# Low parts of thirty weight blocks moved from GpSimd to VectorE at the borders of phases

## Chip, cores and metric

The kernel runs on one core of a Trainium2 chip. The metric is the device time of one execution in microseconds (us); lower is better.

## The reference, cut to what matters

A decoder trunk of two layers on 512 tokens of width 1024 in float32. Each layer is a half-step SwiGLU feed-forward ("ffn"), a token mixer, and a second ffn; every one of the six sub-layers is wrapped in a norm ahead and a norm behind:

```python
h = rmsnorm(x, g[0])
x = x + 0.5 * rmsnorm(swiglu(h, wg, wu, wd), g[1])   # swiglu: (silu(h @ wg) * (h @ wu)) @ wd, 2816 wide
h = rmsnorm(x, g[2])
...                                                  # mixer: z = h @ w_in; scan, gating; y @ w_out
x = x + rmsnorm(y, g[3])
h = rmsnorm(x, g[4])
x = x + 0.5 * rmsnorm(swiglu(h, wg2, wu2, wd2), g[5])
```

## The kernel before

**Split weights.** TensorE multiplies in fp32r, so each operand is split in a high and a low part and a product is three matmuls (high times high, and the two mixed ones). The weights come in blocks of 128x1024. `WeightStream` takes them in one fixed order over the whole kernel: a DMA from SP's queue into one of 4 raw buffers (`load_to`), a cast to `whi` on ScalarE and a subtraction `wlo = raw - whi` (`split`, lines 86 and 87), into one of 8 pairs of buffers (`NW`). The set `early` says for which blocks the subtraction is made by GpSimd; for the others it is VectorE. `prep_to(n)` makes everything up to block n. In three of the ffn phases most gate and up weights come as sevenths of a fast 2x2 scheme; for these blocks VectorE also forms the differences `T` (lines 108 to 119) ahead of the split.

**Phases.** `PLAN` has six: ffn 0/0, mix0, ffn 0/1, ffn 1/0, mix1, ffn 1/1. The 512 tokens are four chunks of 128. A phase ends in `tail` or `out_late` and then `finish`: the output product is summed for one chunk after the other (`some`), and as soon as a chunk is summed its `chain` runs: `post_norm` (a sum of squares on ScalarE, a reciprocal root on VectorE, the residual), then `pre_norm` for the next phase, whose result is `xn`. `rstd` is the reciprocal root: seven instructions on 128x1 columns (lines 450 to 458). `turn` transposes `xn` on TensorE, casts it to `hT_hi` on ScalarE and subtracts to `hT_lo` on VectorE.

**Borders.** The turns of chunks 1 and 2 are put between the last matmuls for chunk 4. Those of chunks 3 and 4 are handed to the next phase as `self.late`. There `lead` makes the first three pairs of weight blocks for tokens 0 to 255 (chunks 1 and 2), turns chunk 3 after the first pair and chunk 4 ahead of the sixth block, and then makes tokens 256 to 511. mix0 has no lead: it makes the gating product of chunk 1, turns chunk 3, goes on with chunk 2 and another product of chunk 1, and turns chunk 4. A paired ffn then forms sums of quarters of `hT` on VectorE (`left_factors`; the last is S3, written back into `hT_lo`).

**Order.** A scheduler orders each engine's instructions by the order in which they are written and by a simulated timeline; each engine then runs its list in order. In the tails TensorE's list is as written. `with tc.issue_after(ins)` adds for each instruction inside, if it is on the same engine as `ins`, that it stands behind `ins` in that engine's list. It leaves the other engines' instructions free.

Of the kernel before, what the change touches and what calls it, by code (L numbers as in the profile page):

```python
# [15 lines left out]
ALU = mybir.AluOpType  # L16
# [13 lines left out]
NW = 8  # L30
# [18 lines left out]
class WeightStream:  # L49
# [4 lines left out]
    def __init__(self, nc, raw_pool, w_pool):  # L54
        self.nc, self.raw_pool, self.w_pool = nc, raw_pool, w_pool
        self.blocks, self.items = [], []
        self.loaded = 0
        self.ready = 0
        self.raw = {}
        self.hi = {}  # L60
        self.lo = {}
        self.t_pool = None
# [327 lines left out]
class Trunk:  # L390
    def __init__(self, ctx, tc, a, out):
        self.ctx, self.tc, self.nc, self.a, self.out = ctx, tc, tc.nc, a, out
        nc = self.nc
        ent = ctx.enter_context
        self.cp = ent(tc.tile_pool(name="cp", bufs=1))
        self.raw_pool = ent(tc.tile_pool(name="rawp", bufs=NRAW))
        self.w_pool = ent(tc.tile_pool(name="wp", bufs=NW))
        self.gp = ent(tc.tile_pool(name="gp", bufs=1))
        self.tp = ent(tc.tile_pool(name="tp", bufs=2))
        self.sp = ent(tc.tile_pool(name="sp", bufs=4))  # L400
        self.ps = ent(tc.tile_pool(name="ps", bufs=4, space=PSUM))

        self.first = {}
        self.ws = WeightStream(nc, self.raw_pool, self.w_pool)
        for ph in PLAN:
            self.first[ph] = len(self.ws.items)
            self.phase_blocks(ph, self.ws)
        self.ws.early = {v + k for v in self.first.values() for k in range(2, 8)} | {0, 1}
        self.ws.early |= {self.first[PLAN[1]] + k for k in range(12, 18)}

        self.x = self.cp.tile([P, NT, D], F32, tag="x", name="x")
        self.hi = self.cp.tile([P, KC, S], F32R, tag="hT_hi", name="hT_hi")
        self.lo = self.cp.tile([P, KC, S], F32R, tag="hT_lo", name="hT_lo")
# [99 lines left out]
    def pre_norm(self, c, gain, nm, cut=D):  # L513

        nc = self.nc
        xn = self.tp.tile([P, D], F32, tag="t", name=f"xn{nm}_{c}")
        ss = self.sumsq(self.x[:, c, :], xn, f"{nm}b{c}")
        r = self.rstd(ss, 1.0 / D, EPS, f"{nm}b{c}")
        nc.vector.scalar_tensor_tensor(xn[:, 0:cut], self.x[:, c, 0:cut], r, gain[:, 0:cut], ALU.mult, ALU.mult)
        if cut < D:  # L520
            nc.gpsimd.tensor_scalar(xn[:, cut:], self.x[:, c, cut:], r, None, ALU.mult)
            nc.gpsimd.tensor_mul(xn[:, cut:], xn[:, cut:], gain[:, cut:])
        return xn
# [55 lines left out]
    def finish(self, acc, some, n, mid, after, ph, nxt, nm):  # L579

        nc, ws = self.nc, self.ws
        xn = {}

        def chain(c):
            self.post_norm(c, acc[c], self.g_post, ph[0] == "ffn", nm, nxt is None)
            if nxt is not None:
                xn[c] = self.pre_norm(c, self.g_pre, nm)

        for c in range(3):
            some(c, 0, n)  # L590
            if c < 2:
                chain(c)
        j = 0
        for c, to in enumerate(mid):
            some(3, j, to)
            if nxt is not None:
                self.turn(c, xn[c], nm)
            if c == 0:
                chain(2)
            j = to  # L600
        some(3, j, n)
        ws.prep_to(after + 4)
        chain(3)
        if nxt is not None:
            self.late = [lambda: self.turn(2, xn[2], nm), lambda: self.turn(3, xn[3], nm)]
# [51 lines left out]
    def lead(self, first, nm, sink, pairs=LEAD):  # L657

        nc, ws = self.nc, self.ws
        w, pg = [], []  # L660
        for i in range(pairs):
            w += [ws.get(first + j, first + j + 1) for j in range(2 * i, 2 * i + 2)]
            pg.append(self.bank2(f"lead{nm}_{i}"))
            if i == 0:
                wh, wl = (v.rearrange("p (k f) -> p k f", f=P) for v in w[0])
                for n, (s, m) in enumerate(((wh, self.hi), (wl, self.hi), (wh, self.lo))):
                    for k in range(KC):
                        nc.tensor.matmul(pg[0][:, 0, 0:256], s[:, k], m[:, k, 0:256],
                                         start=n == k == 0, stop=n == 2 and k == KC - 1)
            else:  # L670
                self.chmajor(pg[i][:, 0], w[2 * i], 0, 256)
            if i == 0:
                self.chmajor(pg[i][:, 1], w[1], 0, 256)
                self.late[0]()
            elif i == pairs - 1:
                with self.tc.issue_after(self.late[1]()):
                    self.chmajor(pg[i][:, 1], w[2 * i + 1], 0, 256)
            else:
                self.chmajor(pg[i][:, 1], w[2 * i + 1], 0, 256)
        for i in range(pairs):  # L680
            ws.prep_to(first + 2 * i + NW)
            for j in range(2):
                self.chmajor(pg[i][:, j], w[2 * i + j], 256, 512)
                ws.drop(first + 2 * i + j)
            sink(i, pg[i])
        ws.prep_to(first + 2 * pairs - 2 + NW)
# [886 lines left out]
```

## Time and profile before

| | |
|---|---|
| median of 3 runs | 1900.11 us (1899.27 to 1902.82) |
| profiled execution | 1899.38 us |
| its span, first to last instruction | 1897.6 us |
| mean granted clock of TensorE | 0.985 of 2.4 GHz |

Engines: PE is TensorE's matmul, PEld its weight load, DVE is VectorE, ACT ScalarE, POOL GpSimd, SP SyncE, whose queue starts the weight loads. L87 is line 87. A row of a timeline gives start and length in us, engine, line, operation, output and inputs, and in brackets how long its engine was idle before it and what ended that.

### The profile page before, as it was taken

The numbers are of one execution on the slowest core, as the hardware profiler recorded it, in microseconds if no ns is written. First come the engines' busy times: TensorE is split into PE (matmuls) and PEld (weight loads), VectorE is DVE, ScalarE is ACT, GpSimd is POOL, SyncE is SP. The second block draws the span as 40 slices with busy tenths as digits, with TensorE's granted clock in tenths as the row PEclk, the third lists the DMA queues.
The fourth block names the chain that finished last, engine by engine and source line by source line (L and its number), as shares of the span: only waits on it lengthen the run. The fifth ranks groups of instructions, "written<-read, shape, count | busy, mean of one in ns | idle before, by whom it ended". The sixth has DMA issues, their size and how long they took to land.

```text
span 1897.6 us, 27701 instructions
## 1 busy us (share of the span) xinstructions
PE 1837.0 (97%) x11192; PEld 1638.0 (86%) x11192; DVE 1220.2 (64%) x1814; ACT 701.1 (37%) x946; POOL 302.0 (16%) x530
## 2 busy tenths in 40 slices
PE   8999999989898999999989999999999989999998
PEld 8888888869787999988889999888988779999886
DVE  5756434284948888853598887428634598887533
ACT  4223224133233544442234444323444334444420
POOL 6037760031402000000110000003122030000000
PEclk9999999989999999999999999999999999999999
DMA  6444432342402233343223335332311132334411
GB/s 224 132 120 147 129 117 89 89 155 92 142 23 89 81 109 112 108 151 98 57 77 91 112 101 166 100 89 81 111 45 45 45 101 88 103 101 133 123 56 45
DMA packets 59602, 193.34 MB, mean 102 GB/s; under 512 B 6577, under 2 KB 13745, under 8 KB 59473
## 3 DMA queue, kind: packets, MB, share of 16 engines
q1 hardware_dynamic: 50544, 182.48, 31.3%
q10 hardware_dynamic: 7680, 5.24, 0.9%
q0 software_dynamic: 1248, 3.84, 0.6%
q8 instruction: 88, 1.44, 0.3%
q14 instruction: 42, 0.34, 0.1%
HBM read 182.10 MB, written 9.44 MB: 101 GB/s over the span
## 4 chain that ended last, share of the span: by engine, by line
PE 89%; DVE 8%; issue 1%; ACT 1%; DMA 0%; DVEq 0%; SPq 0%; ACTq 0%
PE accffn L645 16%; PE accffn L647 8%; PE guffn L543 4%; PE guffn L545 4%; PE guffn L544 4%; PE saffn L848 3%; PE sbffn L848 3%; PE sbffn L847 3%; PE sbffn L849 3%; PE saffn L849 3%; PE saffn L847 3%; PE scffn L848 3%; PE scffn L849 3%; PE scffn L847 3%; PE accmix L645 2%; PE leadffn L544 2%
## 5 line engine op out<-in xcount | busy, mean ns | idle before, releaser
L86 ACT CAST whi<-raw 128x1024 fp32r<-128x1024 f32 x314 | 328.9, 1050 | 610.7 <-PE accffn L647 192.9
L87 DVE TENSOR_TENSOR wlo<-raw,whi 128x1024 fp32r<-128x1024 f32 x270 | 331.8, 1229 | 292.2 <-ACT whi L86 291.7
L87 POOL TENSOR_TENSOR wlo<-raw,whi 128x1024 fp32r<-128x1024 f32 x44 | 106.9, 2454 | 980.7 <-ACT whi L86 971.6
L543 PE MATMUL guffn<-hT_hi,whi 128*128 128x512 f32 x352 | 141.0, 401 | 0.0
L545 PE MATMUL guffn<-hT_hi,wlo 128*128 128x512 f32 x352 | 138.8, 394 | 0.0
L544 PE MATMUL guffn<-hT_lo,whi 128*128 128x512 f32 x352 | 138.1, 392 | 0.0
L848 PE MATMUL saffn<-hT_lo,whi 128*128 128x256 f32 x432 | 122.1, 283 | 0.0
L849 PE MATMUL saffn<-hT_hi,wlo 128*128 128x256 f32 x432 | 122.0, 282 | 0.0
L847 PE MATMUL saffn<-hT_hi,whi 128*128 128x256 f32 x432 | 121.2, 281 | 0.0
L86 ACT CAST whi<-T 128x1024 fp32r<-128x1024 f32 x81 | 85.0, 1050 | 85.9 <-PE saffn L848 43.9
L87 DVE TENSOR_TENSOR wlo<-T,whi 128x1024 fp32r<-128x1024 f32 x81 | 98.9, 1221 | 8.9 <-ACT whi L86 8.9
L545 PE MATMUL leadffn<-hT_hi,wlo 128*128 128x256 f32 x352 | 100.3, 286 | 0.0
L544 PE MATMUL leadffn<-hT_lo,whi 128*128 128x256 f32 x352 | 100.2, 285 | 0.0
L543 PE MATMUL leadffn<-hT_hi,whi 128*128 128x256 f32 x352 | 100.0, 287 | 0.0
L847 PEld LDWEIGHTS saffn<-hT_hi,whi 128*128 128x128 f32 x432 | 82.0, 190 | 0.1
L849 PEld LDWEIGHTS saffn<-hT_hi,wlo 128*128 128x128 f32 x432 | 81.2, 188 | 0.0
L848 PEld LDWEIGHTS saffn<-hT_lo,whi 128*128 128x128 f32 x432 | 80.8, 187 | 0.1
L545 PEld LDWEIGHTS guffn<-hT_hi,wlo 128*128 128x128 f32 x352 | 66.1, 188 | 17.0
L544 PEld LDWEIGHTS guffn<-hT_lo,whi 128*128 128x128 f32 x352 | 66.1, 188 | 15.3
L543 PEld LDWEIGHTS guffn<-hT_hi,whi 128*128 128x128 f32 x352 | 66.1, 188 | 15.0
L543 PEld LDWEIGHTS leadffn<-hT_hi,whi 128*128 128x128 f32 x352 | 67.6, 193 | 0.0
L544 PEld LDWEIGHTS leadffn<-hT_lo,whi 128*128 128x128 f32 x352 | 67.6, 192 | 0.0
(797 smaller groups left out, 5097.2 us busy)
## 6 DMA issues: line engine op xcount, KB each, us to landing
raw<-in_gu_dram SPq DMA_DIRECT2D x108, 512.0 KB, 3.6
raw<-in_wd_dram SPq DMA_DIRECT2D x88, 512.0 KB, 3.6
raw<-in_wg_dram SPq DMA_DIRECT2D x34, 512.0 KB, 3.6
raw<-in_wu_dram SPq DMA_DIRECT2D x34, 512.0 KB, 3.8
raw<-in_even_in_dram SPq DMA_DIRECT2D x12, 512.0 KB, 3.7
raw<-in_odd_tm_dram SPq DMA_DIRECT2D x12, 512.0 KB, 3.6
raw<-in_even_out_dram SPq DMA_DIRECT2D x8, 512.0 KB, 4.4
raw<-in_odd_cm_dram SPq DMA_DIRECT2D x8, 512.0 KB, 3.5
```

Source lines behind the costliest of these rows:

```text
L86: nc.scalar.copy(hi, raw)
L87: (nc.gpsimd if i in self.early else nc.vector).tensor_sub(lo, raw, hi.bitcast(F32))
L543: nc.tensor.matmul(out, sh, mh, start=start, stop=False)
L544: nc.tensor.matmul(out, sh, ml, start=False, stop=False)
L545: return nc.tensor.matmul(out, sl, mh, start=False, stop=stop).ins
L645: nc.tensor.matmul(acc[:, h, :], gh, w[:, h * 512:(h + 1) * 512], start=first, stop=False)
L647: nc.tensor.matmul(acc[:, h, :], gl, wh[:, h * 512:(h + 1) * 512], start=False, stop=stop)
L847: nc.tensor.matmul(o, wh[:, q], ah[k], start=start and k == 0, stop=False, skip_group_check=True)
L848: nc.tensor.matmul(o, wh[:, q], al[k], start=False, stop=False, skip_group_check=True)
L849: nc.tensor.matmul(o, wl[:, q], ah[k], start=False, stop=stop and k == 3, skip_group_check=True)
```

## The change

The set of blocks whose low part GpSimd makes shrinks to the first eight of the kernel and six later ones of mix0; in the five other phases the blocks 2 to 7 go to VectorE. `pre_norm` keeps its last instruction, the one that writes `xn`, in `self.normed`. `finish` prepares six blocks of the next phase, not four, and its VectorE instructions stand behind the `xn` that was written last, which is that of chunk 3; after the last phase it prepares none. `lead` does the same for the blocks behind its first six, behind `xn` of chunk 4.

```diff
-        self.ws.early = {v + k for v in self.first.values() for k in range(2, 8)} | {0, 1}
+        self.ws.early = set(range(8))
         self.ws.early |= {self.first[PLAN[1]] + k for k in range(12, 18)}
...
-        nc.vector.scalar_tensor_tensor(xn[:, 0:cut], self.x[:, c, 0:cut], r, gain[:, 0:cut], ALU.mult, ALU.mult)
+        self.normed = nc.vector.scalar_tensor_tensor(xn[:, 0:cut], self.x[:, c, 0:cut], r, gain[:, 0:cut],
+                                                     ALU.mult, ALU.mult).ins
...
         some(3, j, n)
-        ws.prep_to(after + 4)
+        if nxt is not None:
+            with self.tc.issue_after(self.normed):
+                ws.prep_to(after + 6)
         chain(3)
...
         for i in range(pairs):
-            ws.prep_to(first + 2 * i + NW)
+            with self.tc.issue_after(self.normed):
+                ws.prep_to(first + 2 * i + NW)
             for j in range(2):
                 self.chmajor(pg[i][:, j], w[2 * i + j], 256, 512)
                 ws.drop(first + 2 * i + j)
```

## Rows read from the trace of the kernel before

**Rows 1.** The page, busy time of an engine (share of the span) and instructions.

```profile
PE 1837.0 (97%) x11192; PEld 1638.0 (86%) x11192; DVE 1220.2 (64%) x1814; ACT 701.1 (37%) x946; POOL 302.0 (16%) x530
```

**Rows 2.** Waits of TensorE in the whole span: us in total, times, longest.

```profile
PE ptffn L534 <- DVE xnffn L519: 10.5, 3, 8.5
PE leadffn L668 <- DVE hT_lo L536: 9.6, 2, 6.0
...
PE lead_1m L668 <- DVE hT_lo L536: 3.6, 1, 3.6
```

**Rows 3.** Windows, five borders: length, busy time (instructions) by engine, clock, DMA, GB/s.

```profile
core 0: us, PE busy (x) PEld busy (x) DVE busy (x) ACT busy (x) POOL busy (x), PEclk, DMA share, GB/s
409.47:432.12 22.65, 14.10 (x57) 11.48 (x57) 20.56 (x49) 7.62 (x12) 7.88 (x10) 0.77 0.68 242
577.86:608.57 30.71, 21.76 (x150) 20.35 (x149) 28.39 (x36) 8.25 (x12) 12.45 (x6) 0.89 0.36 118
946.52:970.46 23.94, 18.39 (x129) 17.82 (x128) 22.82 (x34) 6.21 (x9) 7.67 (x4) 0.86 0.33 107
1308.26:1329.93 21.67, 18.07 (x129) 17.86 (x128) 19.64 (x31) 6.20 (x9) 10.76 (x9) 0.84 0.47 145
1526.30:1552.96 26.66, 17.59 (x130) 16.99 (x128) 25.14 (x35) 6.20 (x9) 8.77 (x4) 0.87 0.33 102
sum 125.63, PE 89.91 PEld 84.50 DVE 116.54 ACT 34.48 POOL 47.53; mean PE 17.98 PEld 16.90 DVE 23.31 ACT 6.90 POOL 9.51
```

**Rows 4.** Windows, full clock: 512-column matmuls, then 256-column ones.

```profile
422.52:432.12 9.60, 9.60 (x42) 7.68 (x41) 8.12 (x30) 1.16 (x3) 0.00 (x0) 1.00 0.60 218
...
960.48:969.12 8.64, 8.64 (x73) 8.47 (x71) 8.15 (x20) 2.17 (x3) 0.00 (x0) 1.00 0.04 13
```

**Rows 5.** Behind waits: window at border 3, turn of chunk 3 at border 5.

```profile
952.20:957.90 5.70, 5.70 (x26) 5.70 (x27) 5.41 (x7) 2.94 (x5) 4.63 (x2) 0.50 0.27 87
...
1541.79 1.09 PE L534 MATMUL ptmix<-ident,xnmix 128*128 128x128 f32 x8 [1.66 <-DVE xnmix L519]
```

**Rows 6.** Timeline: an undisturbed norm, a last cast, two square sums of chunk 3.

```profile
926.04 0.15 DVE L450 TENSOR_SCALAR hxffn_1b<-ssffn_1b 128x1 f32<-128x1 f32 x1 [1.22 <-ACT xnffn L480]
...
927.51 1.28 DVE L519 SCALAR_TENSOR_TENSOR xnffn<-x,y2ffn_1b,g_pre 128x1024 f32<-128x1024 f32 x1
...
943.92 1.05 ACT L86 CAST whi<-raw 128x1024 fp32r<-128x1024 f32 x1 [0.32 <-PE accffn L647]
...
573.07 1.01 ACT L480 ACTIVATE tmix<-accmix 128x1024 f32<-128x1024 f32 x1
...
1516.78 1.03 ACT L480 ACTIVATE tmix<-accmix 128x1024 f32<-128x1024 f32 x1
```

**Rows 7.** Timeline of GpSimd and VectorE at borders 3, 1 and 5.

```profile
940.03 9.45 POOL L87 TENSOR_TENSOR wlo<-raw,whi 128x1024 fp32r<-128x1024 f32 x4 [344.48 <-ACT whi L86]
...
940.13 0.14 DVE L452 TENSOR_SCALAR y0ffn_1a<-hxffn_1a 128x1 int32<-128x1 int32 x1
...
944.84 2.33 DVE L456 SCALAR_TENSOR_TENSOR y1ffn_1a<-nt1ffn_1a,y0ffn_1a 128x1 f32<-128x1 f32 x1
...
397.62 2.11 DVE L454 SCALAR_TENSOR_TENSOR nt0ffn_0a<-y0ffn_0a,hxffn_0a 128x1 f32<-128x1 f32 x1
...
413.17 4.87 DVE L519 SCALAR_TENSOR_TENSOR xnffn<-x,y2ffn_0b,g_pre 128x1024 f32<-128x1024 f32 x1
...
1538.10 2.31 DVE L458 SCALAR_TENSOR_TENSOR y2mix_1b<-nt2mix_1b,y1mix_1b 128x1 f32<-128x1 f32 x1
```

**Rows 8.** The page's groups of the subtraction: busy us, mean ns, idle before.

```profile
L87 DVE TENSOR_TENSOR wlo<-raw,whi 128x1024 fp32r<-128x1024 f32 x270 | 331.8, 1229 | 292.2 <-ACT whi L86 291.7
L87 POOL TENSOR_TENSOR wlo<-raw,whi 128x1024 fp32r<-128x1024 f32 x44 | 106.9, 2454 | 980.7 <-ACT whi L86 971.6
```

**Rows 9.** The page's DMA issues: count, KB each, us from issue to landing.

```profile
raw<-in_gu_dram SPq DMA_DIRECT2D x108, 512.0 KB, 3.6
```

**Rows 10.** Timeline: end of the left factors, first matmul that reads S3.

```profile
1001.98 1.22 DVE L796 TENSOR_TENSOR hT_lo<-S3ffn,hT_hi 128x1024 fp32r<-128x1024 f32 x1
...
1011.35 0.28 PE L847 MATMUL sdffn<-hT_hi,whi 128*128 128x256 f32 x1
```

**Rows 11.** Waits of VectorE: us in total, times, longest.

```profile
DVE wlo L87 <- ACT whi L86: 300.6, 165, 10.8
```

## The prediction

> **What bounds the kernel now.** I read the page's busy table first: TensorE is busy for 1837.0 of 1897.6 us [rows 1], so all that a change at the borders of phases can win lies in the 60 us in which it is not, and in matmuls that ran at the lower clock. Then I asked who made TensorE wait: its longest waits are for VectorE, for `xn` before a transpose and for `hT_lo` in the lead [rows 2]. These lie at the five borders between phases: while VectorE and ScalarE norm and turn token chunks 3 and 4, TensorE has only the rest of the old phase and the first products of the new one.
>
> So I cut out, at each border, the stretch from the last matmul before the first such wait to the transposes of chunk 4 [rows 3]; border 1 is ffn 0/0 to mix0, then mix0 to ffn 0/1, ffn 0/1 to ffn 1/0, ffn 1/0 to mix1, mix1 to ffn 1/1. Together they are 125.63 us. TensorE's own work in them, at full clock, is counted: 256-column matmuls start every 0.12 us (73 in 8.64 us), 512-column ones every 0.234 (42 in 9.60 us, eight transposes take 0.8) [rows 4]. Border 1 holds 48 large matmuls and one turn: 12.0 us. Border 2 holds 120 small ones, 12 large, two turns: 18.8. Borders 3 to 5 hold 120 small ones and one turn: 15.2 each. Against the lengths in [rows 3] the excess is 10.6, 11.9, 8.7, 6.5 and 11.4, in sum **49.1 us**. That is the ceiling. Part of it is clock: after the wait of 3.6 us for `hT_lo` at border 3 the granted clock was 0.50, which is 1.2 GHz, for 5.70 us [rows 5].
>
> Why is VectorE late? The Newton steps of a norm are 128x1 instructions. Undisturbed, seven of them take 1.47 us, 0.2 each [rows 6]. While GpSimd makes its four low parts (9.45 us), such a step takes up to 2.33 us, about as long as one low part there (2.45) [rows 7, 8]. The steps that go slow read two SBUF operands; L452, with one, takes 0.14 beside a running low part [rows 7]. I count 28 slow steps, from the one at 397.62 to the one at 1538.10, and two slow `xn`, the longer with 4.87 us in place of 1.28 [rows 6, 7]. Above their undisturbed lengths that is 14.0, 11.6, 12.6, 12.8 and 12.8 us at the five borders: 63.8 us of VectorE time.
>
> **The change, part by part.** *Removed:* the low parts of 30 blocks from GpSimd (six at each of five borders; in the first phase the set is the same eight as before, and mix0's six later blocks stay), and with them the cause of the 63.8 us. *Added to VectorE:* 30 low parts at 1.23 us, next start 1.14 us after the last: 34.2 us [rows 8]. Net relief of VectorE: 29.6 us.
>
> *Moved:* (a) at the borders into a phase from an ffn tail, blocks 0 and 1 are split early as before; 2 to 5 now stand on VectorE behind `xn` of chunk 3. Their casts on ScalarE and their loads are not bound, nor is anything on GpSimd's queue. At mix0's and mix1's ends, all of 0 to 5 stand there, and blocks 0 and 1, which VectorE made earlier, come later. (b) Blocks 6 to 11 of a lead, and the three T differences of a paired ffn, stand behind `xn` of chunk 4; at three borders the T differences ran ahead of it (3.4 us on its path at each). (c) Each low part frees one of four raw buffers, so the load of block i+4 on SP's queue waits for the bound low part; a load takes 3.6 us to land [rows 9], a cast 1.05. (d) In the last phase the skipped `prep_to` has nothing left to prepare.
>
> New times at the borders, from rows:
>
> Border 3. `hT_lo` of chunk 1 no longer waits behind slow steps: its cast ends about 943.6, the lead needs it at 948.4; the 3.6 wait and the slow clock behind it go. Chunk 3: with steps of 0.2 us `x` ends near 942.8; ScalarE's casts run to 944.97 [rows 6], its square sum to 946.2, steps 1.47, `xn` 1.28: **949.0**. Low parts 2 to 5 end at 950.2 to 953.6; TensorE takes block 2 only at 953.1 (lead start 946.52 plus two blocks of 2.88 and a turn), block 3 at 956: no wait. Chunk 4: first product 1.14, steps 1.3, `x` 1.28, square sum 1.25, steps 1.47, `xn` 1.28 from 953.6: 961.3, up to 962.4 if `hT_lo` of chunk 2's turn comes between. TensorE is there at 946.52 + 15.2 = 961.7: a wait of about **0.4**. Border 4 has the same parts: **0.4**. Border 1: `xn` of chunk 3 near 406.2, low part 2 done 407.4, wanted about 406.9: **0.5**; chunk 4's `xn` near 420.5, wanted 422.
>
> Borders 2 and 5, where block 0 waits. The chunk-3 square sum starts at 573.07 and 1516.78 [rows 6]; from there both chains give `xn` near 583.7 and 1526.6, low part 0 near 584.9 and 1527.9. TensorE, no longer held, wants it at 582.5 and 1527.2: waits of **2.4** and **0.7**. After 2.4 us the clock is unknown: it was at 0.50 behind the wait of 3.6 [rows 5], and the turn behind the 1.66 wait ran in 1.09 us, thus at full clock [rows 5]. Bounds 0 and 2.6 (26 matmuls at half clock above); I take **1.5**. Chunk 4 there stands behind up to six low parts, two of them delayed by their loads: **0.4** and **0.6**.
>
> Behind `xn` of chunk 4 the bound low parts are ready at once, while `hT_lo` of chunk 4 becomes ready 2.2 us later and may meet one under way: at most 1.14 at four borders, I take 0.75 each: **3.0**. Further on, S3's split ended at 1003.2 for a matmul at 1011.35 [rows 10]; low parts 6 and 7 and the T differences push it by 5.7 us: 2.5 us are left, so I cost it at nothing; without that cover it is 5.7 at each of three borders.
>
> New waits: 0.5 + 2.4 + 1.5 + 0.4 + 0.4 + 0.4 + 0.7 + 0.6 + 3.0 = **9.9 us**. Gain 49.1 - 9.9 = 39.2. The profiled execution took 1899.38 us, 0.7 below the median 1900.11: 1860.2 there, **1861** beside the median.
>
> VectorE is the engine that takes the work, and it is busy for 116.54 of the 125.63 us of the stretches [rows 3]. Without the 63.8 and the T differences (10.3), with 26 low parts inside (29.6), it has 72.0 us of work in 76.5 us of TensorE work, 94%: hardly any room.
>
> The Trainium skill (Perfetto Trace Analysis, Optimizing Scalar/DVE Operations) says that where VectorE is saturated, work may be moved off it, even to GpSimd, but that between these two a move might not help since they share an SBUF read port. That speaks against loading VectorE here. By the rows the sum is 1861; by that rule VectorE would set the pace and only its net relief would come back, the first rival below.
>
> **Rivals.**
> 1. *VectorE sets the pace of the border.* Its queue is in order, and at 94% each wait for ScalarE (two square sums of 1.2 us a chunk) is lost. Then the stretch shrinks only by the net relief: 1900.1 - 29.6 = **1870.5**. For it: the 93% of now. Against: over half of that is held-up time.
> 2. *The change does not do what it says:* the slow steps have another cause than GpSimd's low parts, such as semaphore traffic with ScalarE's casts, and VectorE merely gets 34.2 us more. Then the 49.1 us stay, and the added low parts are hidden in VectorE's waits for ScalarE or not: about **1900**, or some us more. Against: at all five borders the long steps begin and end with GpSimd's low parts [rows 7].
> 3. *The binding stalls chunk 4* (slower). A bound low part whose cast is late stands at the head of VectorE's queue, and chunk 4's post-norm, pre-norm and turn stand behind it; TensorE waits for the turn. VectorE's longest wait of this kind now is 10.8 us [rows 11]. One such wait on the path at each border gives 5 x 10.8 - 49.1 = +5: **1905**. It decides from 9.8 us per border on. For it: the raw buffers at borders 2 and 5, where load and cast (3.6 + 1.05) follow the release. Against: at borders 1, 3 and 4 the four raws are there before.
>
> **How the numbers follow.** Forecast 0.66, rival 1 0.22, rival 2 0.04 (a quarter of it slower by more than 0.2%), rival 3 0.05, and 0.03 for other reorderings by the scheduler that lose more than 0.2%. The forecast's own range is 1853 (new waits of 2 us) to 1868 (17 us: the 9.9 with 2.6 of clock, 1.14 at four borders and one more VectorE instruction of 1.14 ahead of chunk 4's `xn` at four). Rival 1 with a few us of new waits reaches 1881. So 1853 to 1881 leaves out 0.12 for the two last cases and the rest, and some for sums beyond the edges. Less than 0.2% (3.8 us) can't be told from no change here: faster 0.88, same 0.03, slower 0.09.
>
> **What the profile of the changed kernel would show.** GpSimd without low parts at the five borders (14 instead of 44 in all); no 128x1 step above 0.3 us there; 30 more low parts on VectorE at 1.23 us; TensorE's waits for `xn` of 8.5 us and for `hT_lo` of 6.0 and 3.6 gone [rows 2]; a new wait of 1 to 3 us for `wlo` in the lead behind mix0, and small ones for `xn` of chunk 4. The step from the old lead start to chunk 4's turn should be 15 to 17 us at borders 3 to 5. The prediction is wrong if long waits for `wlo` or for chunk 4's transposes appear, if the paired products begin to wait for S3, or if the steps stay long.

## The result, and the profile after

The changed kernel takes 1877.4 us (median of four runs, 1876.76 to 1878.39) beside 1899.84 for the kernel before on the same chip: a ratio of 0.9879, 95% interval 0.9862 to 0.9896. It is 22.4 us faster; 39 were forecast, for a time of 1861, and the range was 1853 to 1881.

The page of the changed kernel, busy time by engine and VectorE's group of the subtraction (columns as in [rows 1] and [rows 8]):

```profile
PE 1829.0 (98%) x11192; PEld 1629.4 (87%) x11192; DVE 1190.3 (63%) x1844; ACT 701.2 (37%) x946; POOL 231.0 (12%) x500
...
L87 DVE TENSOR_TENSOR wlo<-raw,whi 128x1024 fp32r<-128x1024 f32 x300 | 367.8, 1232 | 293.9 <-ACT whi L86 293.2
```

VectorE has 30 subtractions more than in [rows 8] and is busy for 29.9 us less than in [rows 1]; the forecast of its net relief was 29.6. After 380 us the kernel before has 28 of the 128x1 steps above 0.3 us, the longest 2.51; the changed kernel has none, the longest is 0.22. So the edit did to VectorE what was forecast, within 0.3 us. What TensorE made of it is in the turns of chunk 4 at the five borders (PE timeline of the changed kernel; the kernel before starts the same turns where the windows of [rows 3] end):

```profile
423.96 1.06 PE L535 MATMUL ptffn<-ident,xnffn 128*128 128x128 f32 x8
...
595.13 1.09 PE L535 MATMUL ptmix<-ident,xnmix 128*128 128x128 f32 x8 [2.07 <-DVE xnmix L519]
...
952.73 1.06 PE L535 MATMUL ptffn<-ident,xnffn 128*128 128x128 f32 x8 [0.84 <-DVE xnffn L519]
...
1311.43 1.06 PE L535 MATMUL ptffn<-ident,xnffn 128*128 128x128 f32 x8 [0.66 <-DVE xnffn L519]
...
1527.18 1.09 PE L535 MATMUL ptmix<-ident,xnmix 128*128 128x128 f32 x8 [1.78 <-DVE xnmix L519]
```

Against 432.12, 608.57, 970.46, 1329.93 and 1552.96, chunk 4's turn comes earlier by 8.2, 13.4, 17.7, 18.5 and 25.8 us, and the span ends 22.2 earlier (1897.6 and 1875.4). From one turn to the next that is +8.2, +5.3, +4.3, +0.8, +7.3, and -3.6 after the last. The gain grows over each border, and inside the three paired phases (behind borders 2, 3 and 5) some of it goes again. Where, TensorE's waits say (whole span; us in total, times, longest):

```profile
PE guffn L544 <- DVE S4ffn L815: 8.1, 3, 2.8
PE ptmix L535 <- DVE xnmix L519: 7.6, 4, 2.1
...
PE ptffn L535 <- DVE xnffn L519: 2.3, 3, 0.8
...
PE leadffn L545 <- DVE hT_lo L537: 0.6, 3, 0.2
```

The waits of 8.5, 6.0 and 3.6 us of [rows 2] are gone. The three of `guffn` are new: once in each paired phase the first matmul of the fourth pair of blocks, the first over all 512 tokens, waits for the operation that begins S4. At border 3, VectorE's and TensorE's timelines, and the window behind the wait (columns as in [rows 3]):

```profile
951.30 1.28 DVE L519 SCALAR_TENSOR_TENSOR xnffn<-x,y2ffn_1b,g_pre 128x1024 f32<-128x1024 f32 x1
952.50 2.35 DVE L87 TENSOR_TENSOR wlo<-raw,whi 128x1024 fp32r<-128x1024 f32 x2
954.77 1.22 DVE L108 TENSOR_TENSOR T<-raw,raw 128x1024 f32<-128x1024 f32 x1
...
975.62 1.22 DVE L815 TENSOR_TENSOR S4ffn<-hT_hi,S2ffn 128x1024 f32<-128x1024 f32 x1
```

```profile
976.98 0.75 PE L544 MATMUL guffn<-hT_hi,whi 128*128 128x512 f32 x1 [2.63 <-DVE S4ffn L815]
```

```profile
976.98:980.09 3.11, 3.11 (x7) 2.44 (x8) 3.11 (x4) 0.00 (x0) 0.00 (x0) 0.50 0.36 142
```

The same in the kernel before (VectorE, with its longest idle time between the two, then TensorE):

```profile
969.03 1.28 DVE L519 SCALAR_TENSOR_TENSOR xnffn<-x,y2ffn_1b,g_pre 128x1024 f32<-128x1024 f32 x1
972.61 1.22 DVE L536 TENSOR_TENSOR hT_lo<-ptffn,hT_hi 128x1024 fp32r<-128x1024 f32 x1 [2.29 <-ACT hT_hi L535]
...
989.98 1.22 DVE L811 TENSOR_TENSOR S4ffn<-hT_hi,S2ffn 128x1024 f32<-128x1024 f32 x1
```

```profile
991.52 0.39 PE L543 MATMUL guffn<-hT_hi,whi 128*128 128x512 f32 x1
```

The matmul doesn't read S4. But S4's first operation is the last to read S2, which lies in PSUM, where sums, lead and pairs share the same four tiles of two banks. When the matmul starts, three are taken: by the third pair of the lead, whose last reader starts at 979.02, by S4 and by S3. So I read the wait as that for S2's tile to come free. Before, that operation ended at 991.20, 0.3 us ahead of the matmul, and nothing showed. It came 20.95 us behind the start of chunk 4's `xn`; now it comes 24.32 behind. Three T differences and three low parts more stand between, 6.8 us of work; VectorE had been idle there for 3.2 us in the kernel before and is for 0.3 now, so the delay is 3.4. TensorE's way from chunk 4's turn to this matmul grew from 21.06 (991.52 - 970.46) to 24.25 us (976.98 - 952.73), and in the 3.1 us behind the wait the granted clock is 0.50, which is 1.2 GHz.

### The profile page after: what moved, and what is told of

Same layout as the page of the kernel before. It is cut to its first block, busy times and chain, and to the rows that moved or that the text cites. A ratio compares the mean times of both kernels' runs of the same rounds, so it can differ in the third digit from the quotient of the medians.

```text
span 1875.4 us, 27667 instructions
## 1 busy us (share of the span) xinstructions
PE 1829.0 (98%) x11192; PEld 1629.4 (87%) x11192; DVE 1190.3 (63%) x1844; ACT 701.2 (37%) x946; POOL 231.0 (12%) x500
## 4 chain that ended last, share of the span: by engine, by line
PE 88%; DVE 7%; DMA 2%; issue 2%; ACT 1%; DVEq 0%; SPq 0%; ACTq 0%
PE accffn L648 18%; PE accffn L650 9%; PE guffn L544 5%; PE guffn L546 4%; PE guffn L545 4%; PE accmix L648 3%; PE saffn L852 3%; PE sbffn L852 3%; PE saffn L853 3%; PE sbffn L853 3%; PE sbffn L851 3%; PE saffn L851 3%; PE scffn L852 3%; PE scffn L853 3%; PE scffn L851 3%; PE accmix L650 2%
## 5 line engine op out<-in xcount | busy, mean ns | idle before, releaser
L87 DVE TENSOR_TENSOR wlo<-raw,whi 128x1024 fp32r<-128x1024 f32 x300 | 367.8, 1232 | 293.9 <-ACT whi L86 293.2
```

What stands on the lines that cost most here:

```text
L87: (nc.gpsimd if i in self.early else nc.vector).tensor_sub(lo, raw, hi.bitcast(F32))
```

## Experiments

The kernels were run in three groups, each on one chip with the kernel before beside it (its medians 1900.03, 1900.51 and 1901.77 us); between groups the ratios are compared.

### The change taken apart

**Engine only.** Both bindings undone, the thirty low parts stay on VectorE:

```diff
-        if nxt is not None:
-            with self.tc.issue_after(self.normed):
-                ws.prep_to(after + 6)
+        ws.prep_to(after + 4)
...
-            with self.tc.issue_after(self.normed):
-                ws.prep_to(first + 2 * i + NW)
+            ws.prep_to(first + 2 * i + NW)
```

> The thirty low parts on VectorE as in the changed kernel, but bound to nothing (finish prepares four blocks and lead the rest as in the kernel before). Theory A (GpSimd's low parts hold VectorE's two-operand steps): all 128x1 steps at the borders are 0.2 us or so; by the order of VectorE's list three to six low parts now stand ahead of chunk 3's xn or chunk 4's and T differences with them, 3.4 us and more on each path and half clock behind the waits, so only part of the gain is left: 1885 to 1897. Rival B (the order set by the binding brings the gain, the engine nothing): the steps stay long in places and the time is that of before or worse, 1897 to 1905.

Measured: 1896.14 us, ratio 0.9978 (0.9968 to 0.9988). No 128x1 step is above 0.22 us, and yet only 4 us of the gain are there. The turn of chunk 3 at border 3 now stands behind VectorE's new work (PE timeline; the bracket names the step that VectorE made right behind the `xn` that the turn reads):

```profile
955.48 1.94 PE L535 MATMUL ptffn<-ident,xnffn 128*128 128x128 f32 x8 [6.96 <-DVE nt1ffn_1a L455]
```

Six low parts and three T differences run ahead of chunk 3's `xn` there; the turn waits for 6.96 us and then takes 1.94 us where 1.06 is the length of an undisturbed one.

**Bindings only.** GpSimd's set is that of before, both bindings stay:

```diff
-        self.ws.early = set(range(8))
+        self.ws.early = {v + k for v in self.first.values() for k in range(2, 8)} | {0, 1}
```

> Blocks 2 to 7 of each border back on GpSimd, both bindings of the changed kernel kept (they now hold only the few low parts that VectorE had, and the T differences). Theory A: the long steps are back, 25 to 30 of them at up to 2.3 us, 44 low parts on GpSimd, and the time is 1892 to 1900 (the T differences behind chunk 4's xn may give a few us). Rival B: with the order of the changed kernel most of its gain is there, 1877 to 1885.

Measured: 1893.27 us, ratio 0.9957 (0.9942 to 0.9972), with 25 steps above 0.3 us, up to 2.48. So theory A holds for the steps; but neither half of the change alone brings more than some 7 us of the 22 (8 by the ratio).

**Finish bound, lead free:**

```diff
-            with self.tc.issue_after(self.normed):
-                ws.prep_to(first + 2 * i + NW)
+            ws.prep_to(first + 2 * i + NW)
```

> The changed kernel without the binding in lead; that in finish is kept. By VectorE's list at borders 2, 3 and 5 low parts 6 and 7 and a T difference go back ahead of chunk 4's xn. Theory C (behind chunk 4 the left factors are what is late, since the fourth pair's first matmul waits for S4's first operation): the same VectorE work stands ahead of the left factors as in the changed kernel, so TensorE loses at chunk 4's turn (waits of 3 to 5 us) what it no longer loses at the fourth pair (waits under 1 us): 1876 to 1884. Rival D (the delay of chunk 4's turn comes on top): 3.4 to 5.7 us more at three borders, 1887 to 1894.

Measured: 1892.17 us, ratio 0.9953 (0.9939 to 0.9968): rival D, and theory C's figure for this run was wrong. VectorE's timeline at border 3, from the low parts behind chunk 3's `xn` to chunk 4's residual `x`, and TensorE's turn of chunk 4:

```profile
942.14 4.63 DVE L87 TENSOR_TENSOR wlo<-raw,whi 128x1024 fp32r<-128x1024 f32 x4
...
948.81 1.23 DVE L87 TENSOR_TENSOR wlo<-raw,whi 128x1024 fp32r<-128x1024 f32 x1 [0.71 <-ACT whi L86]
...
952.19 1.23 DVE L108 TENSOR_TENSOR T<-raw,raw 128x1024 f32<-128x1024 f32 x1 [0.70 <-DMA raw<-in_gu_dram]
...
954.43 1.23 DVE L111 TENSOR_TENSOR T<-raw,T 128x1024 f32<-128x1024 f32 x1 [0.69 <-DMA raw<-in_gu_dram]
955.57 1.22 DVE L116 TENSOR_TENSOR raw<-raw,raw 128x1024 f32<-128x1024 f32 x1
956.71 1.28 DVE L507 SCALAR_TENSOR_TENSOR x<-tffn,y2ffn_1a,x 128x1024 f32<-128x1024 f32 x1
```

```profile
962.16 1.94 PE L535 MATMUL ptffn<-ident,xnffn 128*128 128x128 f32 x8 [8.40 <-DVE xnffn L519]
```

Blocks 6 and 7 and the T differences need raw buffers that came free only with low parts 2 to 5. Unbound, they stand at the head of VectorE's list while their loads are on the way, and chunk 4's norms stand behind: `x` starts 14.6 us after low part 2 (942.14 to 956.71), against 6.8 in the changed kernel (940.26 to 947.09). Of the 7.8 us more, 5.7 are the five instructions themselves, 1.14 us each, and 2.1 the idle times for a cast and two loads. In this smaller part it is the mechanism of the prediction's rival 3, here without the binding; the binding in `lead` keeps both parts away.

**Lead bound, finish free:**

```diff
-        if nxt is not None:
-            with self.tc.issue_after(self.normed):
-                ws.prep_to(after + 6)
+        ws.prep_to(after + 4)
```

> The changed kernel without the binding in finish (four blocks prepared there, free); that in lead is kept. By VectorE's list three or four low parts then stand ahead of chunk 3's xn, 3.4 to 4.6 us. If chunk 3's turn is on TensorE's path, as the waits of 0.8 to 1.9 us for it in the changed kernel say, those waits grow to 4 to 6 us at each of the five borders with some half clock behind: 1888 to 1900. If it isn't, the time stays at 1877 to 1880.

Measured: 1877.32 us, ratio 0.9876 (0.9861 to 0.9890), the time of the changed kernel. It isn't the same run of events, though. The turn of chunk 3 at border 1 waits as I had expected,

```profile
416.72 1.94 PE L535 MATMUL ptffn<-ident,xnffn 128*128 128x128 f32 x8 [4.96 <-DVE nt1ffn_0a L455]
```

while only one fourth pair waits for S4 (2.5 us) where three did. Two differences of 5 us or so may have cancelled; a later run tries it.

### What GpSimd's operations do to VectorE's

Two kernels add useless GpSimd work at the thirty blocks, on the changed kernel; in the second the added operation is `tensor_scalar(self.scratch, v, 1.0, None, ALU.mult)`:

```diff
+        for k in range(4 * (i in self.extra)):
+            v = hi.bitcast(F32)[:, 256 * k:256 * k + 224]
+            nc.gpsimd.tensor_sub(self.scratch, v, v)
         self.hi[i], self.lo[i] = hi, lo
```

> The changed kernel, and GpSimd makes at each border, for each of the thirty blocks, four useless subtractions of 128x224 with two SBUF operands (the result goes to a scratch tile and is used by nobody). Theory A (one two-operand instruction of VectorE gets through for each one of GpSimd): the 128x1 steps of the norms meanwhile take about as long as one such subtraction, some 0.5 to 0.6 us instead of 0.2 (a low part of 2.45 us scaled to 224 columns); the time grows to 1880 to 1892. Rival F (the long steps had another cause): steps stay at 0.2, 1877 to 1879.

> As the run with the useless subtractions, but GpSimd's operation is a multiplication by 1 with one SBUF operand, 128x224, four for each of the thirty blocks. If only two-operand work of both engines collides, steps stay at 0.2 us and the time at 1877 to 1879; if any work of GpSimd holds VectorE's two-operand steps, they lengthen to the length of the multiplication as with two operands, and the time with them.

Measured: 1892.53 us with two operands, ratio 0.9959 (0.9945 to 0.9973), and 1883.90 with one, 0.9914 (0.9899 to 0.9929); the changed kernel, run beside them, 1878.70, 0.9884 (0.9869 to 0.9899). The first is half a us above theory A's range. The useless work costs 13.8 and 5.2 us, though nothing waits for its results; VectorE, which does the same work, is busy for 20.7 and 7.7 us more (1211.5 and 1198.5, beside 1190.8). A rival would be that GpSimd's reading keeps the buffers of `whi` from coming free; with two operands no wait of any engine names the useless work, with one a single wait of 0.5 us does. GpSimd's groups and their shortest, median and longest instruction in ns, then steps and low parts of VectorE near border 3, with two operands:

```profile
L90 POOL TENSOR_TENSOR scratch<-whi 128x224 f32<-128x224 f32 x120 | 98.5, 821 | 924.5 <-ACT whi L86 916.0
...
L90 POOL TENSOR_TENSOR scratch<-whi x120: 552/562/1657, 399.5 to 1547.1; 128x224 f32<-128x224 f32 x120
```

```profile
944.54 0.55 DVE L460 SCALAR_TENSOR_TENSOR nt1ffn_1b<-nt0ffn_1b 128x1 f32<-128x1 f32 x1
...
948.24 5.71 DVE L87 TENSOR_TENSOR wlo<-raw,whi 128x1024 fp32r<-128x1024 f32 x4
...
955.70 0.61 DVE L462 SCALAR_TENSOR_TENSOR nt2ffn_1a<-y1ffn_1a,hxffn_1a 128x1 f32<-128x1 f32 x1
```

and with one:

```profile
L90 POOL TENSOR_SCALAR scratch<-whi 128x224 f32<-128x224 f32 x120 | 123.5, 1029 | 904.2 <-ACT whi L86 895.2
...
L90 POOL TENSOR_SCALAR scratch<-whi x120: 769/774/1733, 399.0 to 1539.4; 128x224 f32<-128x224 f32 x120
```

```profile
943.42 5.32 DVE L87 TENSOR_TENSOR wlo<-raw,whi 128x1024 fp32r<-128x1024 f32 x4
...
954.60 0.43 DVE L462 SCALAR_TENSOR_TENSOR nt2ffn_1b<-y1ffn_1b,hxffn_1b 128x1 f32<-128x1 f32 x1
```

With two operands 36 steps are above 0.3 us, the longest 0.61; with low parts of 2.45 us it was 2.51. The longest step shrinks with GpSimd's instruction, which rival F doesn't give. Low parts grow too: four of them take 5.71 and 5.32 us here and 4.63 in the changed kernel. The one-operand work is half-way: 14 steps above 0.3 us, up to 0.43, though GpSimd is busier with it. Both guesses for that run were too simple.

The Trainium skill (SBUF — State Buffer, SBUF: two separate sides) says that VectorE and GpSimd share one pair of SBUF ports as an exclusive lock for the whole instruction, and that a VectorE operation with two SBUF inputs takes part against a GpSimd operation that reads SBUF. The runs agree that GpSimd's work holds VectorE's two-operand steps, with one operand read as with two. That the hold lasts for GpSimd's whole instruction fits the low parts (2.45 us, steps up to 2.51) and, by the median, the small subtractions (0.56 us, steps up to 0.61; their mean of 0.82 holds some of up to 1.66). The multiplications don't show it: their median is 0.77 us, and no step beside them is longer than 0.43.

### The left factors first

In the three paired phases `lead` prepares no more than blocks 6 and 7, and the T differences with all behind them stand behind S4's first operation. All else is the changed kernel:

```diff
-                ws.prep_to(first + 2 * i + NW)
+                ws.prep_to(first + min(2 * i + NW, upto))
...
-            self.lead(first, nm, act)
+            self.lead(first, nm, act, upto=NW if n else 99)
             if n:
                 left = self.left_factors(gtile, fp, nm)
+                with self.tc.issue_after(self.freed):
+                    ws.prep_to(first + 2 * LEAD - 2 + NW)
...
-        V.tensor_sub(s4, a12[0].bitcast(F32), s2)
+        self.freed = V.tensor_sub(s4, a12[0].bitcast(F32), s2).ins
```

> The changed kernel, but in the three paired phases lead prepares only blocks 6 and 7 (still behind chunk 4's xn), and the T differences with all that follows them stand behind S4's first operation. Theory C (that operation frees S2's PSUM bank for the fourth pair): it comes some 3.4 us earlier, the three waits of 2.6 to 2.8 us for it fall below 0.5 us, the half clock behind them goes too: 1866 to 1870. Rival E (VectorE has no room behind the borders, so whatever goes first makes the rest late): waits for T blocks' low parts, or for S3, take their place and the time stays at 1875 to 1880.

> The changed kernel once more beside the other kernels of this call: 1876 to 1879, to compare on one chip. The turn at 24.9 us and the half clock at it, which no edit touches, may differ from the profile already shown (1.1 or 1.9 us long); if so, that 1.5 us of difference is no part of the change.

Measured: 1864.31 us (1864.02 to 1865.75), ratio 0.9811 (0.9797 to 0.9826), 14.4 us below the changed kernel's 1878.70 beside it and 2 below theory C's range. No wait for S4 is left. At border 3 its first operation, the matmul that waited, and chunk 4's turns at borders 2 to 5:

```profile
962.74 1.22 DVE L817 TENSOR_TENSOR S4ffn<-hT_hi,S2ffn 128x1024 f32<-128x1024 f32 x1
```

```profile
593.68 1.09 PE L535 MATMUL ptmix<-ident,xnmix 128*128 128x128 f32 x8 [2.40 <-DVE xnmix L519]
...
947.96 1.06 PE L535 MATMUL ptffn<-ident,xnffn 128*128 128x128 f32 x8 [1.03 <-DVE xnffn L519]
...
969.02 0.39 PE L544 MATMUL guffn<-hT_hi,whi 128*128 128x512 f32 x1
...
1301.83 1.06 PE L535 MATMUL ptffn<-ident,xnffn 128*128 128x128 f32 x8 [0.65 <-DVE xnffn L519]
...
1517.74 1.09 PE L535 MATMUL ptmix<-ident,xnmix 128*128 128x128 f32 x8 [1.91 <-DVE xnmix L519]
```

From chunk 4's turn to the fourth pair it is 21.06 us again (969.02 - 947.96), as in the kernel before. From turn to turn this kernel gains on the one before 9.7, 5.2, 7.6, 5.6 and 7.1 us, and -0.1 after the last (span 1862.5). Against the changed kernel that is 1.5 us more up to border 1, 3.3 more behind border 2, 4.8 behind border 3 and 3.5 behind border 5, and 0.2 less in all elsewhere: the three sum to 11.6. Rival E falls: the same VectorE work in another order makes nothing else late.

The 1.5 us up to border 1 are not the change's: they are there at 33 us, where the fourth turn of the kernel starts (31.79 before, 33.26 in the changed kernel, 31.73 here), and up to there VectorE's list is that of the kernel before. At the first turn of border 1 the profiles lie between 0.1 us ahead of that of the kernel before and 3.8 us behind it. From that turn to the end they take 1503.9 us (before), 1480.2 and 1480.7 (the changed kernel, twice) and 1468.9 (here).

**The same without the binding in finish.**

```diff
-        if nxt is not None:
-            with self.tc.issue_after(self.normed):
-                ws.prep_to(after + 6)
+        ws.prep_to(after + 4)
```

> The kernel with the left factors first, without the binding in finish (four blocks prepared there, free). Without the factors' edit, taking finish's binding away cost nothing in all (1877.3 against 1877.4), but by stretches it lost some 6 us at border 1 and 4 us at border 4 and took less loss at the fourth pairs. If these two only happened to cancel, the loss at the borders is left when the fourth pairs wait for nothing in either kernel: 1872 to 1880. If finish's binding is worth nothing: 1863 to 1866.

Measured: 1869.59 us, ratio 0.9832 (0.9816 to 0.9849), between the two expectations. The wait of 5 us at border 1 is there again. By the ratios the binding in `finish` is worth 4 us in this order (0.0021 of 1900), but the two intervals overlap. From the first turn of border 1 to the end the profile takes 1473.5 us, 4.6 more than with the binding; in the old order the same two figures are 1480.7 without it and 1480.2 with it. That two effects had cancelled is likely, and smaller than I had expected.

**The same with GpSimd's low parts** (the diff of the run with the bindings only, on the kernel with the left factors first):

> The kernel with the left factors first, but blocks 2 to 7 of each border on GpSimd as in the kernel before; all bindings kept. Theory A: with the order at its best the low parts on GpSimd still hold the norms of chunks 3 and 4, so the time is that of the run with the bindings alone, 1890 to 1895, and the move to VectorE is worth some 28 us in this order, against 4 us in the order without bindings. Rival B: the order is what brings it, 1864 to 1875.

Measured: 1890.58 us, ratio 0.9944 (0.9929 to 0.9959). In TensorE's waits those of 8.5 and 3.6 us of before are back (that of 6.0 is not):

```profile
PE ptffn L535 <- DVE xnffn L519: 9.3, 2, 8.5
...
PE leadffn L671 <- DVE hT_lo L537: 3.6, 1, 3.6
PE lead_1m L671 <- DVE hT_lo L537: 3.6, 1, 3.6
```

With the left factors first the move from GpSimd to VectorE is worth 25 us (0.9944 - 0.9811, of 1900), in the order without bindings 4. Order and engine are worth much only together.

**The sixth block later.** On the kernel with the left factors first, `finish` binds five blocks behind chunk 3's `xn` and the sixth behind chunk 4's residual:

```diff
             with self.tc.issue_after(self.normed):
-                ws.prep_to(after + 6)
+                ws.prep_to(after + 5)
         chain(3)
+        if nxt is not None:
+            with self.tc.issue_after(self.resid):
+                ws.prep_to(after + 6)
```

> The kernel with the left factors first, and finish binds only five blocks behind chunk 3's xn; the sixth stands behind the residual of chunk 4, where VectorE has 1.28 us idle for ScalarE's sum of squares. Theory G (what is left at borders 2 to 5 is chunk 4's norms behind the sixth low part, at the mix borders with its cast and its load): the waits of TensorE for chunk 4's xn (2.4 us at border 2, 0.8 and 0.7 at borders 3 and 4) fall by 0.7 to 2.4 us each: 1858 to 1862. Rival: the sixth low part then delays xn of chunk 4 by the 1.14 us instead, or the lead's sixth block waits for it: 1863 to 1867.

Measured: 1863.21 us (1862.92 to 1864.51), ratio 0.9803 (0.9789 to 0.9818); the time is in the rival's range, and its interval overlaps that of the run without this edit, so a gain isn't shown (from the first turn of border 1 on, the one profile of each gives 1465.7 and 1468.9). At the mix borders the waits for chunk 4 did fall as theory G says (ptmix had 8.1 us in all, longest 2.4), at borders 3 and 4 hardly (ptffn had 2.5), and a new one came up:

```profile
PE ptmix L535 <- DVE xnmix L519: 4.6, 4, 1.9
PE ptffn L535 <- DVE xnffn L519: 2.0, 3, 0.8
...
PE ptffn L535 <- DVE nt0sgu L454: 1.2, 1, 1.2
```

## Why the prediction was right in sign and 16 us short

**Right: the cause and VectorE's account.** The slow steps came from GpSimd's low parts: without them there are none, with low parts put back there are 25, and with useless work of shorter instructions there are shorter ones. The rival that the change doesn't do what it says is out.

**Right: the size of borders 2, 3 and 4.** By the prediction's sum, borders 1 to 5 were to give 9.4, 6.9, 7.6, 5.4 and 10.1 us if the 3.0 of `hT_lo` are put on borders 1 to 4 (on 2 to 5, border 1 would be 10.1 and border 5 9.4). With the left factors first, where nothing is given back behind the borders, the five steps from turn to turn measured 9.7, 5.2, 7.6, 5.6 and 7.1. The first two hold a mere shift between them: in TensorE's list for mix0 five matmuls of 512 columns, 1.2 us, now stand behind chunk 4's turn that stood ahead of it, so the turn comes earlier for its place alone. Behind all of them comes `pu`, in the kernel before and with the left factors first:

```profile
444.24 0.63 PE L543 MATMUL pu<-whi,hT_hi 128*128 128x512 f32 x2
```

```profile
435.74 0.64 PE L544 MATMUL pu<-whi,hT_hi 128*128 128x512 f32 x2
```

So border 1 gave 8.5 us. Of these mix0 gives 0.6 back before the first turn of border 2 (569.96 and 562.09), and border 2 gave 7.0. Borders 2, 3 and 4 came out within 0.2 us; border 1 fell short by 0.9 and border 5 by 3.0.

**Wrong: the step that failed.** Of S3's split the prediction says: "low parts 6 and 7 and the T differences push it by 5.7 us: 2.5 us are left, so I cost it at nothing". The cover was read at the wrong reader. I looked for the first matmul that reads S3 [rows 10] and found 2.5 us; but ahead of it the first matmul behind the lead takes over a PSUM tile that the left factors hold, and there only 0.3 us were left. The push measured there is 3.4 us, not 5.7 (24.32 - 20.95), as part of the new work went into time in which VectorE had been idle. It gave waits of 2.6 to 2.8 us at each of the three borders, and slower matmuls behind them: 11.6 us in all, shown by the run with the left factors first. The prediction had priced the case of no cover at 5.7 for each of three borders, but gave it no chance of its own. Its sign of this, paired products that wait for S3, was not seen: the wait came earlier, for S4. In the profiled executions 39.2 us were forecast and 22.2 came; besides the 11.6, the kernel's start took 1.5, border 5 gave 2.8 less, border 1 0.9 less and mix0 took 0.9, while borders 2 to 4 gave 0.9 more.

**Sizes that were off.** At border 5, the chains of chunks 3 and 4 were to cost 0.7 and 0.6 us; the waits are 1.90 and 1.78, 2.4 us more. At border 1, 0.5 and 0.75 were forecast; the waits are 0.84 for chunk 3's turn and 0.7 for a low part. At border 2, 2.4 and 0.4 us of wait and 1.5 for the clock were forecast; the waits are 1.90 and 2.07, and no clock is lost: the granted clock is 1.00 from 570.40 to 595.13, and still from there to 602.00. So the sum of border 2 came out by luck: the clock that wasn't lost paid for chunk 4's longer wait. The first wait went to chunk 3's turn and not to `wlo`, since TensorE's list puts that turn ahead of the low-part product of block 0. The bound low parts ahead of chunk 4's `hT_lo` were put at 3.0; the waits of the lead for it are 0.6 in all.

**The rivals.** "VectorE sets the pace" gives 1870.5, nearer to the time than the forecast, but it isn't what happened: with the left factors first VectorE does the same work and the time is 1864. What fell short was an order. "The binding stalls chunk 4" was not seen; the run without the binding in `lead` shows a stall of this kind, of 2.1 us at border 3, where the binding is missing.

**Not foreseen at all:** that the pieces are worth little alone. The working counted the T differences' place as 3.4 us at three borders. Without the binding in `lead` the loss is 14 us (0.9953 - 0.9879, of 1900): low parts 6 and 7, the T differences and the waits for late loads hold chunk 4's norms as well.

## What to carry to other kernels

When work moves to an in-order engine, ask of each moved instruction what stands behind it in the list, and whether its data are there at its place; what stands behind it pays for its length, and for a late load too. When a chain is pushed back, find the first thing that it releases, buffers and PSUM tiles too, and not only the first reader of its result. And take a change apart before judging its parts: here the engine alone was worth 4 us, the order alone 7, both 22, and with one more binding 36.

## What the runs showed of the hardware

A GpSimd instruction lengthens VectorE's two-operand instructions even when nothing depends on it: 120 subtractions of 0.56 us in the median, with no reader, cost 13.8 us. A GpSimd multiplication by a constant with one operand of 128x224 takes longer than a subtraction with two (774 and 562 ns in the median), and yet lengthens fewer VectorE steps (14 and 36 above 0.3 us).

TensorE kept its full clock behind waits of 1.90, 2.07 and 2.40 us for chunks 3 and 4 (granted clock 1.00 in the 6 us behind each), while at the fourth pair, behind 2.63 us, it was 0.50 for 3.1 us. The length of the wait alone doesn't tell the two apart: in the changed kernel a turn at 24.86 us, behind a wait of 2.19, ran at 0.50, though the clock had been 1.00 ahead of the wait (20.00 to 22.60). Nor does a turn of full length show that the clock stays: without the binding in `lead`, a turn at border 4 behind a wait of 3.68 us ran at 1.00, and the 1.94 us behind it at 0.57 (windows of that run):

```profile
1321.72:1322.78 1.06, 1.06 (x10) 1.06 (x11) 0.00 (x0) 0.00 (x0) 0.00 (x0) 1.00 0.00 0
1322.78:1324.72 1.94, 1.94 (x13) 1.94 (x12) 0.86 (x1) 1.01 (x1) 0.00 (x0) 0.57 0.64 264
```
